# HGRN scores inside a 128-token tile: two full-width matmuls and four masked copies against seven matmuls of 32 stationary columns and one masked copy

## The chip, the cores and the metric

The kernel runs on one core of one Trainium2 chip. The metric is the device time of one execution in microseconds (us). Engines are named as the profile names them: PE is TensorE's matmuls, PEld its weight loads, DVE VectorE, ACT ScalarE, POOL GpSimd, SP SyncE, which only issues DMAs. A matmul holds a stationary operand (up to 128 columns, loaded by a weight load) and streams a moving operand past it; an output row of the matmul belongs to a stationary column, an output column to a moving column.

## The reference, cut to what matters

One decoder layer over 512 tokens: an input projection split over a gated linear recurrence (HGRN2, 4 heads of 128) and a block attention (MoBA), an output projection, cross-attention, a squared-ReLU MLP. The change touches only the HGRN2 heads:

```python
HGRN_CHUNK = 32
b = jnp.cumsum(gc, axis=3)                  # log decay inside a chunk of 32 tokens
q_t = qc * jnp.exp(b)
k_t = kc * jnp.exp(-b)
k_end = kc * jnp.exp(b_last - b)
A = jnp.where(causal, jnp.einsum('bhncd,bhnsd->bhncs', q_t, k_t), 0.0)
o_intra = jnp.einsum('bhncs,bhnsv->bhncv', A, vc)
decay = jnp.exp(b_last[..., 0, :])
def step(state, xs):
    q_n, k_n, v_n, dec_n = xs
    o_n = jnp.einsum('bhcd,bhdv->bhcv', q_n, state)
    new_state = dec_n[..., None] * state + jnp.einsum('bhsd,bhsv->bhdv', k_n, v_n)
    return new_state, o_n
```

## The kernel before, in words

**Tiles and heads.** A chunk is 32 tokens, and the kernel groups four chunks to a tile of 128 tokens, so a head has NT = 4 tiles. Inside a tile, the recurrence between its four chunks is unrolled into scores: a source token s and a target token c of the same tile have a score that goes into AT (source in the partitions, target in the columns). For a target in the source's own chunk the score is `kt` (k_t) against q_t; for a later chunk it is `kend` (k_end, kept in the buffer `Fz`) against q_t times the decay of the chunks in between. The states S pass from tile to tile only.

**What a head does.** `hgrn_pre` makes `kt`, `kend` and the small decay tables (`dc`, `ee`, `pp`, `ss`, `dt`). `ev_q` takes the projected queries of a head out of PSUM and makes, for each pair of tiles g, the buffer `qx[g]`: 128 columns of q_t per tile, and behind them copies of the later chunks' queries that are already multiplied by one or two decays, 224 columns per tile in all. `hgrn_out` is a Python generator whose pieces are the steps between its `yield`s: it transposes `ke` (tile `ket`, copied to `kets` by ACT), then makes the scores, then the tile states `pd` and `S`, then the outputs `ho`, and then normalises them (`osq`, `osh`, `osl`, `on`).

**The scores before.** Per tile there is one matmul of `kt` (128 stationary columns) against 128 columns of q_t, into the tile `a1`, and one of `kend` (128 stationary columns) against the 192 columns `32:224` of `qx`, into `a2`; the profile shows both tiles as `a`. All operands are float32, and the profile records each such matmul as two weight loads and two matmul passes. Four masked copies pick the valid blocks into AT, which was zeroed once at the start: one over all four tiles of `a1` with the mask `m0`, and for each pair of tiles three of `a2` with the masks `m1`, `m2`, `m3`, so 1 + 2 x 3 = 7 DVE instructions (COPY_PREDICATED) per head. The four masks are columns of `cst`, a 128x448 constant that ACT's queue loads from memory.

**What sets the order.** All big projections (`hf`, `hi`, `hq`, `mv`, `mkq`, `hg`, `wo`, `xq`, `xo` and the MLP's `X` and `Y`) go through `mm`, which issues one matmul and, after every 4 of them (GAP), calls `pump`: it looks for a waiting generator whose inputs are ready and issues one piece of it, up to its next `yield`. "Ready" is judged by `Pace`, a bookkeeping of estimated costs in the kernel's own Python: a float32 matmul is charged 0.215 us or 0.00168 us per moving column, whichever is more, and an input counts as ready when it is done by that bookkeeping and 2.5 us more have passed (SLACK). So the order of instructions on every engine is fixed when the program is built. The weights of a projection are split into a high part `wh` (ACT) and a low part `wl` (DVE) two units ahead of their use (SPLIT_AHEAD).

**On the lines.** Nearly every instruction is issued through one helper, L118, so the profile's groups are told apart by the names of tiles.

Of the kernel before, what the change touches and what calls it, by code (L numbers as in the profile page):

```python
# [7 lines left out]

F32 = mybir.dt.float32
F32R = mybir.dt.float32r  # L10
I32 = mybir.dt.int32
# [4 lines left out]
P = 128  # L16
# [7 lines left out]
CHUNK = 32  # L24
# [3 lines left out]
C_MASK, C_M0, C_M1, C_M2, C_M3, C_END = 0, 128, 256, 352, 416, 448  # L28
# [97 lines left out]
def hybrid_layer(ctx: ExitStack, tc: tile.TileContext, xT, memT, ws, vecs, consts, rots, out):  # L126
    nc = tc.nc
    pace = Pace()
    V, A, PE = (pace.engine(e, t) for e, t in ((nc.vector, "dve"), (nc.scalar, "act"), (nc.tensor, "pe")))
# [8 lines left out]
    fp = first.enter_context(tc.tile_pool(name="first", bufs=1, reuse_waits="tile"))  # L138
# [6 lines left out]
    def s8(dtype, name):  # L145
        return sp.tile([P, 4, T], dtype, tag="s8", name=name, bufs=N8)
# [3 lines left out]
    def s2(dtype, name, shape=(T,)):  # L150
        if name.startswith(EARLY2):
            return ep.tile([P, *shape], dtype, tag="e2", name=name, bufs=N2E)
        return sp.tile([P, *shape], dtype, tag="s2", name=name, bufs=N2)
# [14 lines left out]
    def side_bank(name):  # L168
        return pside.tile([P, T], F32, tag="ps", name=name)
# [263 lines left out]
    def start(g, key, wait=0.0):  # L433
        rec = [g, None, key]
        made[key] = rec
        side.append(rec)
        set_wait(rec, wait)
# [22 lines left out]
    def drain(key):  # L460

        rec = made[key]
        n = 0
        while any(r is rec for r in side):
            step(rec)
            n += 1
            assert n < 1000, key

    def smm(o, l, r, start=True, stop=True):

        PE.matmul(o, l, r, start=start, stop=stop, skip_group_check=True)

    def transpose(o, i):
        PE.transpose(o, i, ident)
# [64 lines left out]


    vec = cpool.tile([P, V_END], F32, name="vec")
    cst = fp.tile([P, C_END], F32, name="cst")
    rot = fp.tile([P, 2, T], F32, name="rot")
    cmask = fp.tile([P, T], F32, name="cmask")
    scan_mask = fp.tile([P, T], F32, name="scan_mask")
# [13 lines left out]
    def by_k(t):  # L559
        return t.rearrange("p (h k c) -> p h k c", h=HEADS, k=2)  # L560
# [30 lines left out]
    nc.gpsimd.memset(eps, EPS)  # L591
    make_identity(nc, ident)
    nc.gpsimd.tensor_copy(ones_r, ones)
    ATs = []
    for i in range(2):
        t = fp.tile([P, NT, P], F32, name=f"AT{i}")
# [62 lines left out]
    for k in range(5, KT):  # L659
        square_x(k)  # L660
    del raws[0]
    A.dma_start(cst, consts)
    A.dma_start(cmask[:, T - P:], consts[:, C_MASK:C_MASK + P])
    A.dma_start(rot[:32], rots)

    def rsqrt_of(dst, src, div):

        A.activation(dst, src, AF.Ln, bias=eps, scale=1.0 / div)
        A.activation(dst, dst, AF.Exp, scale=-0.5)

    def column_sums(ps, src, n, name, later=None):

        hi, lo = s2(F32R, f"{name}h"), s2(F32R, f"{name}l")
        A.activation(hi[:, :n], src, AF.Copy)
        V.tensor_sub(lo[:, :n], src, hi[:, :n].bitcast(F32))
        yield [lo[:, :n]]
        if later:
            yield later
        smm(ps[:, :n], ones_r, hi[:, :n], True, False)
        smm(ps[:, :n], ones_r, lo[:, :n], False, True)  # L680
# [45 lines left out]
    for k in range(KT):  # L726
# [7 lines left out]
        for hs in ((0, 1), (2, 3)) if k == 0 else ((0,), (1,), (2,), (3,)):  # L734
            w = {h: [by_k(t[k // 2])[:, h, k % 2] for t in (his, los)] for h in hs}
# [11 lines left out]

    Vh = s8(F32, "Vh")
    on = s8(F32, "on")
    m0 = cst[:, C_M0:C_M0 + P].bitcast(I32)  # L750
    m1 = cst[:, C_M1:C_M1 + 96].bitcast(I32)
    m2 = cst[:, C_M2:C_M2 + 64].bitcast(I32)
    m3 = cst[:, C_M3:C_M3 + 32].bitcast(I32)
    lnf = s8(F32, "lnf")
    A.activation(lnf, Fz, AF.Ln)
    head = {}
# [45 lines left out]
    def hgrn_out(h, qx, q4):  # L802
        H = head[h]
        kt, kend, ke, dt_ = H["kt"], H["kend"], H["ke"], H["dt"]
        AT = ATs[h % 2]

        yield [ke]
        pt = side_bank("ket")
        for t in range(3):
            transpose(pt[:, t * P:(t + 1) * P], ke[:, t * P:(t + 1) * P])  # L810
        ket = s2(F32, "kets")
        A.activation(ket[:, :3 * P], pt[:, :3 * P], AF.Copy)
        yield [qx[0][:, :, :P], qx[1][:, :, :P]]
        pa = side_bank("a1")
        for t in range(NT):
            smm(pa[:, t * P:(t + 1) * P], kt[:, t * P:(t + 1) * P], qx[t // 2][:, t % 2, 0:P])
        V.copy_predicated(AT, m0[:, None, :].to_broadcast([P, NT, P]), pa.rearrange("p (t c) -> p t c", c=P))
        for g in range(2):
            yield [qx[g]]
            pb = side_bank("a2")  # L820
            for t in range(2 * g, 2 * g + 2):
                smm(pb[:, (t % 2) * 192:(t % 2 + 1) * 192], kend[:, t * P:(t + 1) * P], qx[g][:, t % 2, 32:224])
            pv = pb[:, :384].rearrange("p (t c) -> p t c", c=192)
            for m, a, w, c in ((m1, 0, 96, 32), (m2, 96, 64, 64), (m3, 160, 32, 96)):
                V.copy_predicated(AT[:, 2 * g:2 * g + 2, c:], m[:, None, :].to_broadcast([P, 2, w]), pv[:, :, a:a + w])
        yield [ket[:, :3 * P]]
        pd = side_bank("pd")
        for t in range(3):
            smm(pd[:, t * P:(t + 1) * P], ket[:, t * P:(t + 1) * P], Vh[:, t, h * P:(h + 1) * P])
        S = s2(F32, f"S{h}")  # L830
        A.activation(S[:, :P], pd[:, :P], AF.Copy)
        for t in range(1, 3):
            V.scalar_tensor_tensor(S[:, t * P:(t + 1) * P], S[:, (t - 1) * P:t * P], dt_[:, t:t + 1],
                                   pd[:, t * P:(t + 1) * P], op0=ALU.mult, op1=ALU.add)
        yield [S[:, :3 * P], AT, q4]
        po = side_bank("ho")
        for t in range(NT):
            smm(po[:, t * P:(t + 1) * P], Vh[:, t, h * P:(h + 1) * P], AT[:, t, :], True, t == 0)
            if t:
                smm(po[:, t * P:(t + 1) * P], S[:, (t - 1) * P:t * P], q4[:, t * P:(t + 1) * P], False, True)  # L840
        sq = s2(F32, "osq")
        A.activation(sq, po, AF.Square)
        pn = side_bank("on")
        yield from column_sums(pn, sq, T, "os")
        rsqrt_of(sq, pn, P)
        V.tensor_mul(on[:, h, :], po, sq)
# [11 lines left out]
    def ev_q(h, acc):  # L858
        drain(("pre", h))
        H = head[h]  # L860
        qx = [s2(F32, f"qx{g}", (2, 224)) for g in range(2)]
        rbeb = H["rbeb"].rearrange("p (t c) -> p t c", c=P)
        av = acc.rearrange("p (t c) -> p t c", c=P)
        q4 = s2(F32, "q4")
        for g in range(2):
            t0 = 2 * g
            q = qx[g]
            V.tensor_mul(q[:, :, :P], av[:, t0:t0 + 2], rbeb[:, t0:t0 + 2])
            V.tensor_mul(q[:, :, P:P + 64].rearrange("p t (c s) -> p t c s", s=CHUNK),
                         q[:, :, 64:P].rearrange("p t (c s) -> p t c s", s=CHUNK),  # L870
                         H["dc"][:, t0:t0 + 2, 1:3, None].to_broadcast([P, 2, 2, CHUNK]))
            V.tensor_mul(q[:, :, P + 64:P + 96], q[:, :, 96:P],
                         H["ee"][:, t0:t0 + 2, 1:2].to_broadcast([P, 2, CHUNK]))
            V.tensor_mul(q4[:, t0 * P:(t0 + 2) * P].rearrange("p (t c s) -> p t c s", c=4, s=CHUNK),
                         q[:, :, :P].rearrange("p t (c s) -> p t c s", s=CHUNK),
                         H["pp"][:, t0:t0 + 2, :, None].to_broadcast([P, 2, 4, CHUNK]))
        start(hgrn_out(h, qx, q4), ("out", h))

    fm_stage(u, x_act, T, ev_q, "hq", ONE * 4)
    u += 4  # L880

# [474 lines left out]
    g = [s8(F32, f"g{i}") for i in range(8)]  # L1356
# [263 lines left out]
    for p, (name, begins, after) in enumerate(PLAN):  # L1620
# [3 lines left out]
        for j in range(8):  # L1624
            i, c, n = 8 * p + j, j // 4, j % 4
# [114 lines left out]
```

## Time and profile before

| | |
|---|---|
| time, median of 3 runs (lowest, highest) | 729.71 us (729.28, 729.94) |
| the profiled execution's own time | 729.77 us |
| its span (first to last recorded work) | 727.7 us |
| granted TensorE clock | 0.996 |
| PE busy | 719.3 us (99%), 4210 recorded matmul passes |
| PEld busy | 636.6 us (87%) |
| DVE busy | 573.0 us (79%) |
| ACT busy | 445.9 us (61%) |
| POOL busy | 80.9 us (11%) |

Busy PE time is the union of modelled matmul spans, and neighbouring matmuls overlap in it. What a matmul really occupies is read from the distance between the starts of neighbouring rows of the timeline. The HGRN heads' scores lie between 60 and 127 us of the span; the float32r matmuls of `hq` and `mv` run around them.

### The profile page before, as it was taken

The numbers are of one execution on the slowest core, as the hardware profiler recorded it, in microseconds if no ns is written. First come the engines' busy times: TensorE is split into PE (matmuls) and PEld (weight loads), VectorE is DVE, ScalarE is ACT, GpSimd is POOL, SyncE is SP. The second block draws the span as 40 slices with busy tenths as digits, with TensorE's granted clock in tenths as the row PEclk, the third lists the DMA queues.
The fourth block names the chain that finished last, engine by engine and source line by source line (L and its number), as shares of the span: only waits on it lengthen the run. The fifth ranks groups of instructions, "written<-read, shape, count | busy, mean of one in ns | idle before, by whom it ended". The sixth has DMA issues, their size and how long they took to land.

```text
span 727.7 us, 11176 instructions
## 1 busy us (share of the span) xinstructions
PE 719.3 (99%) x4210; PEld 636.6 (87%) x4210; DVE 573.0 (79%) x932; ACT 445.9 (61%) x676; POOL 80.9 (11%) x96
## 2 busy tenths in 40 slices
PE   9999999999999999999999999999999999999996
PEld 7888888888888888888888999999999888888885
DVE  6799556999888677677578888787888899987885
ACT  7882458455787577666565755556546655546672
POOL 1421222000000000000011111211011100110000
PEclk9999999999999999999999999999999999999998
DMA  9999689974557865463758587899889975998523
GB/s 297 285 293 309 151 169 216 363 255 127 136 176 207 250 204 174 152 196 116 232 126 162 146 205 197 216 254 264 255 227 262 318 264 179 279 274 252 181 79 116
DMA packets 63989, 155.84 MB, mean 214 GB/s; under 512 B 5280, under 2 KB 21152, under 8 KB 63424
## 3 DMA queue, kind: packets, MB, share of 16 engines
q1 hardware_dynamic: 47920, 116.43, 45.9%
q0 software_dynamic: 14592, 37.75, 28.6%
q10 hardware_dynamic: 1424, 0.95, 0.4%
q8 instruction: 33, 0.54, 0.3%
q14 instruction: 20, 0.16, 0.1%
HBM read 153.02 MB, written 48.23 MB: 277 GB/s over the span
## 4 chain that ended last, share of the span: by engine, by line
PE 97%; DMA 1%; DVE 0%; SPq 0%; ACT 0%; DVEq 0%; issue 0%
PE X L118 25%; PE Y L118 19%; PE xo L118 8%; PE mkq L118 6%; PE xq L118 6%; PE wo L118 6%; PE hg L118 3%; PE mv L118 3%; PE memX L118 3%; PE hq L118 3%; PE hi L118 3%; PE hf L118 2%; PE memY L118 2%; PE xs L118 2%; PE a L118 1%; PE po L118 1%
## 5 line engine op out<-in xcount | busy, mean ns | idle before, releaser
L118 DVE TENSOR_TENSOR wl<-wr,wh 128x1024 fp32r<-128x1024 f32 (+1 forms) x138 | 165.8, 1205 | 35.4 <-ACT wh L118 25.6
L118 ACT ACTIVATE wh<-wr 128x1024 fp32r<-128x1024 f32 (+1 forms) x138 | 142.7, 1042 | 73.7 <-DMA wr<-in_ws_dram 17.2
L236 POOL DMA_DIRECT2D u<-in_ws_dram x32 | 28.6, 893 | 353.4 <-PE memX L118 108.6
L118 PE MATMUL X<-op,wh 128*128 128x512 f32 (+1 forms) x264 | 62.9, 385 | 0.0
L118 PEld LDWEIGHTS X<-op,wh 128*128 128x128 f32 x264 | 47.2, 189 | 8.4
L118 PE MATMUL Y<-op,wh 128*128 128x512 f32 x192 | 47.2, 391 | 0.0
L118 PE MATMUL Y<-OS,wh 128*128 128x256 f32 x256 | 47.0, 283 | 0.0
L118 PE MATMUL X<-OS,wh 128*128 128x256 f32 x256 | 46.4, 283 | 0.0
L118 PEld LDWEIGHTS Y<-op,wh 128*128 128x128 f32 x192 | 35.0, 189 | 6.5
L118 PEld LDWEIGHTS Y<-OS,wh 128*128 128x128 f32 x256 | 40.0, 192 | 0.0
L118 PEld LDWEIGHTS X<-OS,wh 128*128 128x128 f32 x256 | 39.9, 192 | 0.0
L118 ACT ACTIVATE g<-t 128x512 f32<-128x512 f32 x32 | 19.0, 625 | 30.7 <-DVE t L118 30.7
L118 PE MATMUL X<-OS,wl 128*128 128x256 f32 x128 | 36.2, 283 | 0.0
L118 PE MATMUL Y<-OS,wl 128*128 128x256 f32 x128 | 36.2, 283 | 0.0
L118 PEld LDWEIGHTS X<-op,wl 128*128 128x128 f32 x256 | 33.5, 191 | 1.7
L118 PE MATMUL X<-op,wl 128*128 128x256 f32 x256 | 34.1, 282 | 0.0
L118 DVE TENSOR_TENSOR op<-g,op 128x1024 fp32r<-128x1024 f32 x24 | 29.3, 1220 | 2.8 <-ACT op L118 2.8
L118 ACT ACT_TABLE_LOAD x22 | 28.2, 1283 | 4.2 <-issue 1.8
L118 ACT ACTIVATE op<-g 128x1024 fp32r<-128x1024 f32 x28 | 29.3, 1045 | 0.5 <-PE X L118 0.5
L118 ACT ACTIVATE t<-X 128x256 f32<-128x256 f32 x32 | 11.3, 376 | 27.3 <-PE X L118 27.2
L118 PEld LDWEIGHTS Y<-op,wl 128*128 128x128 f32 x192 | 25.3, 191 | 1.3
L118 PE MATMUL Y<-op,wl 128*128 128x256 f32 x192 | 25.7, 282 | 0.0
(349 smaller groups left out, 2076.3 us busy)
## 6 DMA issues: line engine op xcount, KB each, us to landing
wr<-in_ws_dram SPq DMA_DIRECT2D x87, 512.0 KB, 5.4
u<-in_ws_dram POOLq DMA_DIRECT2D x32, 512.0 KB, 7.0
wr<-u SPq DMA_DIRECT2D x32, 512.0 KB, 4.6
u<-in_ws_dram SPq DMA_DIRECT2D x16, 512.0 KB, 10.5
wr<-m SPq DMA_DIRECT2D x16, 512.0 KB, 3.5
m<-in_ws_dram POOLq DMA_DIRECT2D x12, 512.0 KB, 8.8
m<-in_ws_dram POOLq DMA_DIRECT2D x16, 256.0 KB, 5.9
wA<-in_ws_dram SPq DMA_DIRECT2D x8, 512.0 KB, 5.5
```

The source lines that it names most:

```text
L118: return f(*args, **kw)
L236: return nc.gpsimd.dma_start(dst, src, accum_op=ALU.add, max_dma_last_dim=4 * D)
```

## The change

The scores of a tile are cut by bands of 32 source tokens. Each of the four chunks c of a tile has its own matmul of `kt`'s 32 columns, which writes the 32 partitions of that chunk in one tile `a`: columns from the tile's start to the end of chunk c, so 32, 64, 96 and 128 moving columns. The first three chunks have a second matmul, of `kend`'s 32 columns, which writes the same 32 partitions for the later chunks, with 96, 64 and 32 moving columns. In the program each of these carries a tile size of 128 rows by 32 columns and the column position 0, 32, 64 or 96 of its partitions; every other matmul of the program is 128 by 128. So a tile has seven matmuls, a head 28, and all of a head's are issued in one piece together with the three transposes of `ket`. One masked copy per head then takes the whole of `a` under the mask `causal`, which POOL makes at the start (a memset and a select); `cst` and its load are gone, and so are the six narrow masked copies per head.

`qx` is 256 columns per tile, with the twice-decayed queries of the last chunk in its last 32 columns, so that the three blocks which chunk 0 needs lie at equal distances.

```diff
+    make_upper_triangular(nc, causal, 1.0, diag=True)
...
-    A.dma_start(cst, consts)
...
-        yield [ke]
+        yield [ke, qx[0], qx[1]]
...
-        yield [qx[0][:, :, :P], qx[1][:, :, :P]]
-        pa = side_bank("a1")
+        pa = side_bank("a")
         for t in range(NT):
-            smm(pa[:, t * P:(t + 1) * P], kt[:, t * P:(t + 1) * P], qx[t // 2][:, t % 2, 0:P])
+            q = qx[t // 2][:, t % 2].rearrange("p (a s) -> p a s", s=CHUNK)
+            for c in range(4):
+                rows, own = slice(c * CHUNK, (c + 1) * CHUNK), slice(t * P + c * CHUNK, t * P + (c + 1) * CHUNK)
+                smm(pa[rows, t * P:own.stop], kt[:, own], q[:, :c + 1])
+            for c in range(3):
+                rows, own = slice(c * CHUNK, (c + 1) * CHUNK), slice(t * P + c * CHUNK, t * P + (c + 1) * CHUNK)
+                smm(pa[rows, own.stop:(t + 1) * P], kend[:, own], q[:, c + 1::3][:, :3 - c])
         V.copy_predicated(AT, m0[:, None, :].to_broadcast([P, NT, P]), pa.rearrange("p (t c) -> p t c", c=P))
-        for g in range(2):
-            yield [qx[g]]
-            pb = side_bank("a2")
-            for t in range(2 * g, 2 * g + 2):
-                smm(pb[:, (t % 2) * 192:(t % 2 + 1) * 192], kend[:, t * P:(t + 1) * P], qx[g][:, t % 2, 32:224])
-            pv = pb[:, :384].rearrange("p (t c) -> p t c", c=192)
-            for m, a, w, c in ((m1, 0, 96, 32), (m2, 96, 64, 64), (m3, 160, 32, 96)):
-                V.copy_predicated(AT[:, 2 * g:2 * g + 2, c:], m[:, None, :].to_broadcast([P, 2, w]), pv[:, :, a:a + w])
...
-        qx = [s2(F32, f"qx{g}", (2, 224)) for g in range(2)]
+        qx = [s2(F32, f"qx{g}", (2, 2 * P)) for g in range(2)]
...
-            V.tensor_mul(q[:, :, P + 64:P + 96], q[:, :, 96:P],
+            V.tensor_mul(q[:, :, P + 96:], q[:, :, 96:P],
```

On PE, at the first head's scores during the projection `hq` of the third head, the order before (`a` from `kt` for pairs of tiles; the matmuls from `Fz` come later, in two more pieces, after `hq` matmuls each):

```order
L118 MATMUL ket<-ident,ke_546 128x128 x3
L118 MATMUL hq_761<-xlo_127,wh_631 128x512
L118 MATMUL hq_761<-xhi_125,wl_632 128x512
L118 MATMUL hq_761<-xhi_125,wh_631 128x512
L118 MATMUL hq_761<-xlo_127,wh_631 128x512
L118 MATMUL a_791<-qx_694,kt_439 128x128 x2
L118 MATMUL a_791<-qx_695,kt_439 128x128 x2
L118 MATMUL hq_761<-xhi_125,wl_632 128x512
```

and the order now, up to the end of the first tile's scores; 21 more matmuls of the same form, of the other three tiles, follow before the next `hq` matmul:

```order
L118 MATMUL hq_764<-xhi_124,wl_644 128x512
L118 MATMUL ket<-ident,ke_549 128x128 x3
L118 MATMUL a<-qx_697,kt_442 32x32
L118 MATMUL a<-qx_697,kt_442 32x64
L118 MATMUL a<-qx_697,kt_442 32x96
L118 MATMUL a<-qx_697,kt_442 32x128
L118 MATMUL a<-qx_697,Fz 32x96
L118 MATMUL a<-qx_697,Fz 32x64
L118 MATMUL a<-qx_697,Fz 32x32
```

The three pieces of a head (two tiles' worth of `Fz` matmuls in each of the last two) have become one piece of 3 transposes and 28 matmuls, with no `hq` matmul inside it, and it stands some 13 `hq` matmuls earlier in the third head's projection.

On DVE, at the first head's masked copies, the order before (`AT_152` is the first head's, `AT_154` the second's; `S` are the tile states, `wl` a weight's low part, `qx` and `q` the third head's queries):

```order
L118 COPY_PREDICATED AT_152<-cst,a_791 128x512
L118 TENSOR_TENSOR qx_798<-hq_761,eb_568 128x2x128
L118 TENSOR_TENSOR wl_892<-wr_709,wh_891 128x1024
L118 TENSOR_TENSOR qx_798<-qx_798,dc_603 128x2x64
L118 TENSOR_TENSOR qx_798<-qx_798,ee_599 128x2x32
L118 TENSOR_TENSOR q_800<-qx_798,pp_600 128x256
L118 TENSOR_TENSOR qx_799<-hq_761,eb_568 128x2x128
L118 COPY_PREDICATED AT_152<-cst,a_821 128x2x96
```

and the order now (`AT_156` is the first head's, `AT_158` the second's):

```order
L118 COPY_PREDICATED AT_156<-causal,a 128x512
L118 SCALAR_TENSOR_TENSOR S_815<-S_815,dt_477,pd 128x128 x2
L118 COPY_PREDICATED AT_158<-causal,a 128x512
L118 TENSOR_TENSOR wl_995<-wr_712,wh_994 128x1024
L118 TENSOR_TENSOR osl<-osq,osh 128x512
L118 TENSOR_TENSOR qx_884<-hq_764,eb_571 128x2x128
```

The second head's masked copy now stands right behind the first head's states and ahead of the third head's queries, with a weight's split and the first head's normalisation queued behind it.

More of the change, by code (lines that the diff above doesn't have):

```diff
@@ L6 @@
 from concourse._compat import with_exitstack
-from concourse.masks import make_identity
+from concourse.masks import make_identity, make_upper_triangular
 F32 = mybir.dt.float32
@@ L541, in hybrid_layer @@
     vec = cpool.tile([P, V_END], F32, name="vec")
-    cst = fp.tile([P, C_END], F32, name="cst")
+    causal = fp.tile([P, P], F32, name="causal")
     rot = fp.tile([P, 2, T], F32, name="rot")
@@ L749, in hybrid_layer @@
     on = s8(F32, "on")
[L750 to L753, printed above, removed]
+    m0 = causal.bitcast(I32)
     lnf = s8(F32, "lnf")
```

## The prediction

> **What bounds the kernel now.** First the page's busy times and its chain of work that ended last, then that chain in order of time, and then what PE waited for.
>
> ```profile
> PE 719.3 (99%) x4210; PEld 636.6 (87%) x4210; DVE 573.0 (79%) x932; ACT 445.9 (61%) x676; POOL 80.9 (11%) x96
> ```
>
> ```profile
> PE 97%; DMA 1%; DVE 0%; SPq 0%; ACT 0%; DVEq 0%; issue 0%
> ```
>
> ```profile
> 3.15 6.32 DMA wr<-in_ws_dram
> 10.59 1.24 DVE wl L118
> 11.87 13.70 PE hf L118 x59
> ```
>
> ```profile
> PE warm L118 <- POOL eps L591: 1.0, 1, 1.0
> PE hf L118 <- DVE wl L118: 0.2, 1, 0.2
> ```
>
> After 11.9 us the path is PE alone, and the two waits PE has in all are over by then. So the time is a sum of PE issue distances, and the other engines count only where they would make PE wait. The stretch with the HGRN heads, by the windows view (columns PE, PEld, DVE, ACT, POOL, clock, DMA share, GB/s), leaves DVE a third of its time free:
>
> ```profile
> 60.00:127.00 67.00, 67.00 (x366) 58.01 (x365) 42.52 (x98) 35.49 (x48) 14.06 (x13) 1.00 0.87 206
> ```
>
> **The price of a pass.** PE's timeline at the first head's scores (start, length, and the matmuls of one row):
>
> ```profile
> 67.81 1.05 PE L118 MATMUL a<-qx,kt 128*128 128x128 f32 x8
> 68.62 0.47 PE L118 MATMUL hq<-xhi,wl 128*128 128x512 f32 x1
> 68.93 0.39 PE L118 MATMUL hq<-xhi,wh 128*128 128x512 f32 x1
> 69.16 0.39 PE L118 MATMUL hq<-xlo,wh 128*128 128x512 f32 x1
> 69.39 0.40 PE L118 MATMUL hq<-xhi,wl 128*128 128x512 f32 x1
> 69.63 0.82 PE L118 MATMUL a<-qx,Fz 128*128 128x192 f32 x4
> 70.15 0.52 PE L118 MATMUL hq<-xhi,wh 128*128 128x512 f32 x1
> 70.51 0.40 PE L118 MATMUL hq<-xlo,wh 128*128 128x512 f32 x1
> ```
>
> An `hq` matmul takes 0.23 us from start to start (68.93, 69.16, 69.39). From the start of the eight `kt` passes to the second `hq` behind them are 1.12 us; less one `hq`, 0.89 / 8 = 111 ns per pass of 128 moving columns. For the `Fz` passes 70.51 - 69.63 - 0.23 = 0.65, / 4 = 162.5 ns at 192 columns. The difference, 51.5 ns for 64 columns, is 0.80 ns per moving column, and I extend that line downwards: 85 ns at 96 columns, 60 at 64, 34 at 32.
>
> **Part 1, the scores on PE, removed and added.** Before, a tile takes two passes of each kind, 2 x 111 + 2 x 162.5 = 547 ns; 16 tiles (4 heads of 4) make 8.75 us. Now a tile streams 32 + 64 + 96 + 128 + 96 + 64 + 32 = 512 columns, against 320, in 14 passes. One round of the seven is 2 x 34 + 2 x 60 + 2 x 85 + 111 = 469 ns, and the two rounds of passes 938. What no row of before shows is how much of this runs at the same time, since every matmul in it takes the whole width. The ends:
>
> - Nothing overlaps: 16 x 0.938 = 15.0 us, so +6.3 us.
> - The four bands of 32 columns work fully by themselves: each band streams 128 columns per round, for instance 2 x (34 + 85) = 238 ns in a tile; 16 x 0.238 = 3.8 us, so -4.9 us.
> - Matmuls start in program order, each as soon as its own band is free: the second pass of a matmul waits for the first (same band), but the first pass of the next matmul (another band) starts beside that second pass. Two run at a time, and a tile takes one round, 469 ns: 16 x 0.469 = 7.5 us, so -1.25 us.
>
> I take the third, because every row of PE's timeline before starts in program order and nothing suggests that it would do so less here. [...] All bands here use all 128 rows. [...]
>
> ```profile
> L118 PEld LDWEIGHTS a<-qx,kt x32: 187/192/193, 67.6 to 102.5; 128*128 128x128 f32 x32
> L118 PE MATMUL a<-qx,kt x32: 271/275/275, 67.8 to 102.6; 128*128 128x128 f32 x32
> ```
>
> A load of 192 ns and a pass of 275 fit into 111 ns per pair, so loads do run beside passes. What a load would cost if the bands undid that is the fourth case, below.
>
> **Part 2, changing the array's shape.** Each head's burst now changes from 128x128 to 128x32 and back, 8 changes in all. The trace has only changes of data type, and they cost nothing beyond the 111 ns above: that is the lower bound, 0. Upper bound: a pass is recorded at 275 ns but handed on after 111, so 164 ns of it is a tail that the next pass normally covers. If a change has to let it run out, and then load weights with nothing beside it (111 ns more, what a pair takes), it costs 275 ns. I take the tail alone, 164 ns: 8 x 0.164 = +1.3 us; the ends are 0 and 2.2. [...]
>
> **Part 3, the masked copies.** By the groups of DVE in 60 to 130 us (count, busy us, mean ns, idle time before them) and by the waits of the whole span:
>
> ```profile
> L118 DVE COPY_PREDICATED AT<-cst,a 128x192 f32<-128x192 int32 x8 | 3.0, 375 | 2.8 <-PE a L118 2.8
> L118 DVE COPY_PREDICATED AT<-cst,a 128x512 f32<-128x512 int32 x4 | 3.0, 742 | 5.2 <-PE a L118 5.2
> L118 DVE COPY_PREDICATED AT<-cst,a 128x128 f32<-128x128 int32 x8 | 2.4, 299 | 0.2
> L118 DVE COPY_PREDICATED AT<-cst,a 128x64 f32<-128x64 int32 x8 | 1.8, 226 | 0.2
> ```
>
> ```profile
> DVE AT L118 <- PE a L118: 8.0, 7, 3.0
> ```
>
> The 24 narrow copies, 3.0 + 2.4 + 1.8 = 7.2 us of DVE, go; the four wide ones stay. DVE is not on the path and PE waits for none of it, so this is worth 0. What remains is a wait of DVE for the whole burst, with a weight's `wl` (1.2 us) behind it, by the order shown; that weight is used two units later, over 10 us at 24 `hq` matmuls of 0.23 us each. Cost 0; if the cover failed, PE would wait for one `wl`, 1.2 us, at one place.
>
> **Part 4, the order.** The kernel's own bookkeeping charges the burst 28 x 0.215 = 6.0 us, and by my sum it takes about 2. So what follows is issued up to 4 us too early, against a margin of 2.5. The nearest reader is `pd`, four `hq` behind the burst: 1.9 + 0.3 + 0.9 = about 3 us after the transposes, and it needs ACT's copy `kets`:
>
> ```profile
> 67.07 0.49 ACT L118 ACTIVATE kets<-ket 128x384 f32<-128x384 f32 x1 [3.75 <-PE ket L118]
> 89.97 0.47 ACT L118 ACTIVATE kets<-ket 128x384 f32<-128x384 f32 x1
> ```
>
> For the first head ACT stood waiting 3.75 us for it, so the copy is in time. For a later one ACT came to it from other work, and there PE could wait; I put 0 and at most 1 us.
>
> **Part 5, the start.** The load of `cst` is issued at 15.9 us, after the DMA wait of PE's path had ended, and POOL's two small operations come behind `ones_r` and `eps`, which PE's first matmuls need:
>
> ```profile
> 15.92 0.35 ACTq L118 DMA_DIRECT2D cst<-in_consts_dram  x1
> 1.43 0.28 POOL L593 CAST ones_r<-ones 128x128 fp32r<-128x128 f32 x1
> ```
>
> Both are worth 0.
>
> **Sum.** -1.25 + 1.3 = +0.05 us on the profiled execution's 729.77 us (727.7 of span and 2.1 around it): 729.8. The median of the three runs is 0.06 below that execution, so 729.8 stands for either. With the change of shape between 0 and 2.2 and up to 1 us of waits this case runs from 728.5 to 731.7. A measurement of this kernel tells about 0.2%, 1.5 us, from no change: this is "the same".
>
> **The rivals.**
>
> *One after the other* (slower). The bands do not run together, and 512 columns simply replace 320: +6.3, and the changes of shape 1.3: 737.4 us. For it: every recorded matmul before took PE alone, and the line of 0.80 ns per column holds between the two shapes there are. It decides early: with the changes of shape at 1.3, a tile that takes more than 0.56 us instead of 0.469 already puts the sum beyond 1.5 us (16 x (0.56 - 0.547) + 1.3); with free changes of shape the point is 0.64 us.
>
> *Bands by themselves* (faster). The seven matmuls spread over four bands with 128 columns each: -4.9 + 1.3 = -3.6, 726.1 us; 724.8 if a change of shape is free. For it: the four bands are evenly filled, and no data passes between them. Against it: starts in program order. [...]
>
> *A pass has a floor* (slower). Four matmuls with one moving column each show what a pass costs when it streams nothing:
>
> ```profile
> 31.83 0.95 PE L118 MATMUL nc<-ident,rb 128*128 128x1 f32 x8
> 32.64 0.47 PE L118 MATMUL hi<-wh,xlo 128*128 128x512 f32 x1
> 32.95 0.39 PE L118 MATMUL hi<-wh,xhi 128*128 128x512 f32 x1
> ```
>
> (32.95 - 31.83 - 0.23) / 8 = 111 ns, as much as with 128 columns. Those passes load 128 stationary columns. If it is the load's columns that cost, 32 of them cost a quarter, and nothing changes; if it is the pair of instructions, or a load that finds no cover, the 224 passes take 224 x 0.111 = 24.9 us, +16.1, and with the changes 747 us. [...]
>
> That the change does not do what it says is not a rival: the bands carry their own column positions in the program.
>
> **How the numbers follow.** Chances: the forecast 0.42, one after the other 0.28, bands by themselves 0.20, the floor 0.08, waits behind a burst that cost over 1.5 us 0.02. The forecast's case gives "same" 0.35, and its ends 0.05 slower and 0.02 faster. So faster 0.20 + 0.02 = 0.22, the same 0.35, slower 0.28 + 0.08 + 0.02 + 0.05 = 0.43. The likeliest single case is the forecast, 729.8 us with its own range 728.5 to 731.7; the range has to reach to both neighbours, from 725.5 (between the two ends of the bands by themselves) to 738.0 (one after the other, with half of the dearer change of shape). It leaves out the floor and a little at each end.
>
> **What would show it.** In the timeline after, the first `hq` start behind a burst tells all: the burst of 28 matmuls (56 passes) spans about 1.9 us from its first start if two run at a time, 1.0 if the bands run by themselves, 3.75 one after the other, 6.2 with the floor. A change of shape shows as a gap of about 0.16 us ahead of the burst's first pass and of the `hq` behind it. DVE's busy time should fall by 7 us. PE should show no wait for `kets`, `S` or AT; one over 1.5 us would make part 4 wrong.

## The result and the profile after

The changed kernel takes 725.53 us (median of 6 runs, 724.92 to 726.31) against 729.83 us for the kernel before (6 runs, 729.28 to 730.39). The ratio is 0.9942 with a 95% interval of 0.9929 to 0.9955: faster by 0.58%, or 4.3 us. The forecast had been no change, 729.8 us. (In the repeat of the changed kernel further down, one execution of five took 1188.4 us at a granted clock of 0.557; its ratio is that of the other four.)

The page after: the busy times, and the shares of the chain that ended last.

```profile
PE 714.9 (99%) x4370; PEld 631.5 (87%) x4370; DVE 567.2 (78%) x908; ACT 443.6 (61%) x674; POOL 81.4 (11%) x98
...
PE 99%; DVE 0%; ACT 0%; DVEq 0%; issue 0%; POOL 0%; POOLq 0%
```

PE is the whole path, as it was. It has 160 more recorded passes (224 of the narrow scores for 64 wide ones) and is busy 4.4 us less. DVE is busy 5.8 us less. All that PE waited for is the start; the wait of 0.2 us of `hf` for `wl`, which the kernel before had there, is not in this profile:

```profile
PE warm L118 <- POOL eps L591: 1.0, 1, 1.0
```

PE's timeline at the second head's scores (start, length, matmuls of one row; a row joins neighbours that use the same tiles and prints the shape of its first, so a row of several `kt` passes can hold several widths):

```profile
68.13 0.49 PE L118 MATMUL ket<-ident,ke 128*128 128x128 f32 x3
68.55 0.32 PE L118 MATMUL a<-qx,kt 128*32 128x32 f32 x5
68.64 0.25 PE L118 MATMUL a<-qx,Fz 128*32 128x96 f32 x1
68.64 0.28 PE L118 MATMUL a<-qx,kt 128*32 128x64 f32 x2
68.69 0.22 PE L118 MATMUL a<-qx,Fz 128*32 128x64 f32 x1
68.70 0.27 PE L118 MATMUL a<-qx,kt 128*32 128x128 f32 x1
68.72 0.26 PE L118 MATMUL a<-qx,Fz 128*32 128x96 f32 x4
...
68.95 0.26 PE L118 MATMUL a<-qx,Fz 128*32 128x96 f32 x4
...
69.18 0.26 PE L118 MATMUL a<-qx,Fz 128*32 128x96 f32 x4
...
69.59 0.51 PE L118 MATMUL hq<-xhi,wh 128*128 128x512 f32 x1
69.93 0.40 PE L118 MATMUL hq<-xlo,wh 128*128 128x512 f32 x1
70.17 0.40 PE L118 MATMUL hq<-xhi,wl 128*128 128x512 f32 x1
```

Three things can be read here. The rows 68.72, 68.95 and 69.18 are the same place in three neighbouring tiles: a tile takes 0.23 us (0.228 by the single records of the trace, which the rows join). The burst, from the first score at 68.55 to the `hq` start at 69.59, is 1.04 us; the prediction had listed 1.0 for bands by themselves and 1.9 for two at a time. And the starts are not in program order: the program has all eight `kt` passes of a tile ahead of its first `Fz` pass, but one `Fz` pass starts after five of them, and the other three `kt` passes start later. The single records of the first tile show the bands side by side (start in ns after 68.550):

```
band 0:  0 (32 columns)   53 (32)    85 (96)   170 (96)   next tile 253
band 1:  7 (64)           87 (64)   143 (64)   199 (64)   next tile 255
band 2: 14 (96)          120 (96)   203 (32)   231 (32)   next tile 263
band 3: 20 (128)         154 (128)                        next tile 263
```

Each band goes through its own list at its own pace.

**The sum after.** From the start of `ket` to the second `hq` behind it are 69.93 - 68.13 = 1.80 us. Less one `hq`, 0.23, and less the transposes (before, by the two rows below, 67.12 - 66.55 - 0.23 = 0.34), the burst with both changes of shape costs 1.23 us per head. Before, a head paid 0.89 + 0.65 + 0.65 = 2.19 us for the same scores. The difference, 4 x 0.96 = 3.8 us, is what the scores save on PE by this sum. The rows of before, in its timeline:

```profile
66.55 0.49 PE L118 MATMUL ket<-ident,ke 128*128 128x128 f32 x3
66.79 0.49 PE L118 MATMUL hq<-xlo,wh 128*128 128x512 f32 x1
67.12 0.39 PE L118 MATMUL hq<-xhi,wl 128*128 128x512 f32 x1
```

Of the 1.23 us, four tiles are 0.91; I put the other 0.32 down to the two changes of shape, 0.16 each on average.

The two timelines also give the gain whole. These are the first `hq` matmul and the first `X` matmul, before and then after; all the scores lie between them:

```profile
51.36 0.39 PE L118 MATMUL hq<-xhi,wh 128*128 128x512 f32 x1
400.66 0.40 PE L118 MATMUL X<-OA,wh 128*128 128x256 f32 x2
...
50.85 0.39 PE L118 MATMUL hq<-xhi,wh 128*128 128x512 f32 x1
396.09 0.40 PE L118 MATMUL X<-OA,wh 128*128 128x256 f32 x2
```

From `hq` to `X` are 349.30 us before and 345.24 after, 4.06 less (345.29 in the repeat of the changed kernel). So the sum of 3.8 misses about 0.25 us of this stretch. The other 0.5 us by which the changed kernel's profile is ahead were there before the first `hq`, and no score had run by then.

### The profile page after: what moved, and what is told of

Its sections match the earlier page's. It is cut to its first block, busy times and chain, and to the rows that moved or that the text cites. A ratio compares the mean times of both kernels' runs of the same rounds, so it can differ in the third digit from the quotient of the medians.

```text
span 723.1 us, 11459 instructions
## 1 busy us (share of the span) xinstructions
PE 714.9 (99%) x4370; PEld 631.5 (87%) x4370; DVE 567.2 (78%) x908; ACT 443.6 (61%) x674; POOL 81.4 (11%) x98
## 4 chain that ended last, share of the span: by engine, by line
PE 99%; DVE 0%; ACT 0%; DVEq 0%; issue 0%; POOL 0%; POOLq 0%
PE X L118 25%; PE Y L118 19%; PE xo L118 8%; PE mkq L118 6%; PE xq L118 6%; PE wo L118 6%; PE hq L118 3%; PE hf L118 3%; PE hg L118 3%; PE mv L118 3%; PE memX L118 3%; PE hi L118 3%; PE memY L118 2%; PE xs L118 2%; PE sc L118 1%; PE po L118 1%
```

## The experiments

**One band.** Theory A: the four bands work side by side. Rival B: a narrow pass is cheap by itself. Rival C: the gain is not PE's.

```diff
-                rows, own = slice(c * CHUNK, (c + 1) * CHUNK), slice(t * P + c * CHUNK, t * P + (c + 1) * CHUNK)
+                rows, own = slice(0, CHUNK), slice(t * P + c * CHUNK, t * P + (c + 1) * CHUNK)
...
-        V.copy_predicated(AT, m0[:, None, :].to_broadcast([P, NT, P]), pa.rearrange("p (t c) -> p t c", c=P))
+        V.copy_predicated(AT[:CHUNK], m0[:CHUNK, None, :].to_broadcast([CHUNK, NT, P]), pa[:CHUNK].rearrange("p (t c) -> p t c", c=P))
```

The second loop's `rows` (the three dots) is changed in the same way.

> All seven matmuls of a tile write the same 32 partitions, so they all use the first column band of the array; everything else, the order of instructions included, stays as in the changed kernel. Only the first band's scores reach AT, so the scores of the other three bands are left out. Theory A (the four bands of 32 columns work side by side, each at its own pace, so a tile takes as long as its longest band, 0.228 us in the changed kernel's trace): without other bands the passes queue, 14 passes of about 28, 56, 86 or 110 ns are 0.90 us per tile, 16 x (0.90 - 0.228) = 10.8 us more than the changed kernel, 736.3 us. Rival B (a pass of 32 stationary columns is simply cheap, because its weight load is a quarter): the same 725.5 us as the changed kernel. Rival C (the gain comes from the copies or from the start, not from TensorE): 725.5 us too.

Measured: 736.41 us (736.09 to 737.46), 1.0097 of the kernel before (1.0080 to 1.0114). The first burst, in PE's timeline:

```profile
63.88 0.75 PE L118 MATMUL a<-qx,kt 128*32 128x32 f32 x8
64.47 0.50 PE L118 MATMUL a<-qx,Fz 128*32 128x96 f32 x6
64.80 0.72 PE L118 MATMUL a<-qx,kt 128*32 128x32 f32 x8
...
67.59 0.50 PE L118 MATMUL hq<-xhi,wh 128*128 128x512 f32 x1
```

Now the eight `kt` passes come before the six `Fz` passes. The first tile takes 0.92 us (63.88 to 64.80), each later one 0.90 by the single records, and the burst 3.71. The order of instructions on PE is the changed kernel's; only the band differs, and with it the partitions that are written. So B and C fall: without the four bands the same passes are 6.7 us slower than the kernel before. Going from one band to four makes a tile about 4 times as fast (0.90 against 0.228 us).

**Two bands.**

```diff
-                rows, own = slice(c * CHUNK, (c + 1) * CHUNK), slice(t * P + c * CHUNK, t * P + (c + 1) * CHUNK)
+                rows, own = slice(c % 2 * CHUNK, (c % 2 + 1) * CHUNK), slice(t * P + c * CHUNK, t * P + (c + 1) * CHUNK)
...
```

The second loop's `rows` is changed in the same way, and the masked copy takes the first 64 partitions alone.

> Chunks 0 and 2 write the first 32 partitions, chunks 1 and 3 the second 32, so two of the four bands work; the scores of the upper two bands are left out of AT. If a tile takes its longest band: 2 x (28 + 86 + 86 + 28) = 456 ns, twice the changed kernel's, 16 x 0.228 = 3.65 us more, 729.3 us. If two bands already carry all that the array takes at once (four bands are no better than two): 725.6 us. If less than two bands' worth runs together: up to the 736.4 us of the run with one band.

Measured: 729.24 us (728.79 to 729.57), 0.9995 (0.9985 to 1.0004). In PE's timeline of the first burst:

```profile
64.11 0.53 PE L118 MATMUL a<-qx,kt 128*32 128x32 f32 x8
...
66.05 0.50 PE L118 MATMUL hq<-xhi,wh 128*128 128x512 f32 x1
```

The burst is 1.94 us. So the time follows the longest band's list, 1.04, 1.94 and 3.71 us for four, two and one.

**The bands outermost.** How far ahead does PE look?

```diff
-        for t in range(NT):
-            q = qx[t // 2][:, t % 2].rearrange("p (a s) -> p a s", s=CHUNK)
-            for c in range(4):
+        for c in range(4):
+            for t in range(NT):
+                q = qx[t // 2][:, t % 2].rearrange("p (a s) -> p a s", s=CHUNK)
...
-            for c in range(3):
+                if c < 3:
```

> The same 28 matmuls per head, but the four tiles of band 0 first, then those of band 1, 2, 3: 8 matmuls, 16 passes, stand in one band before the next band's first. Theory A with a look-ahead that reaches all 56 passes: each band starts at once, the burst stays 1.0 us, 725.5 us. Theory A with starts in program order (a pass can't start before the one ahead of it has): the bands run one after the other, 4 x 4 x 0.228 = 3.65 us per head, 10.4 us more, 736 us. A look-ahead of a few passes lies between, and the starts of band 1 against the end of band 0 in the trace give its depth.

Measured: 734.00 us (733.47 to 734.38), 1.0059 (1.0044 to 1.0074): neither end. In PE's timeline of the first burst:

```profile
63.74 0.25 PE L118 MATMUL a<-qx,kt 128*32 128x32 f32 x2
63.82 0.33 PE L118 MATMUL a<-qx,Fz 128*32 128x96 f32 x2
...
64.44 0.25 PE L118 MATMUL a<-qx,kt 128*32 128x32 f32 x3
64.50 0.25 PE L118 MATMUL a<-qx,Fz 128*32 128x96 f32 x1
64.53 0.22 PE L118 MATMUL a<-qx,kt 128*32 128x64 f32 x1
64.59 0.28 PE L118 MATMUL a<-qx,Fz 128*32 128x64 f32 x3
...
66.85 0.50 PE L118 MATMUL hq<-xhi,wh 128*128 128x512 f32 x1
```

The row of 64 columns at 64.53 is band 1's second pass; it starts before band 0's last, so a band does start ahead of the program's order, but only late in the other's list. The single records show how late. Bands 0, 1 and 2 have 16 passes each here, and the next band's first pass starts 6 ns after the 13th of the band ahead of it: 715 after 709 ns, 1415 after 1409, 2126 after 2120. Each time three passes of the band ahead had not started: in this run a band started when 13 of the 16 passes of the band ahead had. What held it until then, no trace shows. The burst is 3.12 us, 4 x (3.12 - 1.04) = 8.3 us more than the changed kernel; measured are 8.5 more.

**Band by band inside a tile.** The edge of what was seen there: four passes of one band in a row.

```diff
             for c in range(4):
...
                 smm(pa[rows, t * P:own.stop], kt[:, own], q[:, :c + 1])
-            for c in range(3):
-                rows, own = slice(c * CHUNK, (c + 1) * CHUNK), slice(t * P + c * CHUNK, t * P + (c + 1) * CHUNK)
-                smm(pa[rows, own.stop:(t + 1) * P], kend[:, own], q[:, c + 1::3][:, :3 - c])
+                if c < 3:
+                    smm(pa[rows, own.stop:(t + 1) * P], kend[:, own], q[:, c + 1::3][:, :3 - c])
```

> Inside each tile both matmuls of a band stand together (four passes of band 0, then four of band 1, four of band 2, two of band 3), tile after tile. The run with the bands outermost showed band 1 starting when three passes of band 0 ahead of it had not started yet. If that is the rule (each band holds up to three passes that wait, and only a fourth one holds up what stands behind it): four passes of a band hold up nothing, the tile stays at 0.228 us and the burst at 1.04, 725.6 us. If passes start in program order, as the prediction had it: about 0.62 us per tile, 16 x 0.39 = 6.3 us more, 731.9 us.

Measured: 726.34 us (725.48 to 726.38), 0.9950 (0.9933 to 0.9966). In PE's timeline of the first burst:

```profile
64.62 0.34 PE L118 MATMUL a<-qx,kt 128*32 128x32 f32 x5
...
65.73 0.50 PE L118 MATMUL hq<-xhi,wh 128*128 128x512 f32 x1
```

The burst is 1.10 us, 0.06 more than expected. By the single records band 0 keeps its 228 ns per tile, but in every tile one pass of band 3 is followed by the next only after 132 to 134 ns; in the changed kernel, from band 3's second pass on, that is 109 to 110. So its last pass starts 94 ns later than there: four in a row do hold band 3 up a little. The rest of the 0.7 us over the expected time is within the interval; the profile has two short waits of PE ahead of all scores, 0.5 us (`hf` for `wl`) and 0.4 (`hq` for `Vh`), in a part that the edit does not touch. Program order is out by 5.6 us.

**Four pieces.**

```diff
                 smm(pa[rows, own.stop:(t + 1) * P], kend[:, own], q[:, c + 1::3][:, :3 - c])
+            if t < NT - 1:
+                yield [qx[t // 2]]
```

> A head's burst is cut into four pieces, one per tile, with four projection matmuls between them: 24 more changes of the array's shape in all. If a change costs the tail of a pass, 0.164 us: +3.9 us, 729.5 us, and all of the change's gain is gone. If a change is free and the 0.32 us around a burst are something that a head pays once: 725.5 us.

Measured: 729.79 us (729.61 to 730.19), 1.0002 (0.9993 to 1.0011), so the cuts eat the whole gain. In PE's timeline:

```profile
65.01 0.39 PE L118 MATMUL hq<-xhi,wl 128*128 128x512 f32 x1
65.24 0.39 PE L118 MATMUL hq<-xhi,wh 128*128 128x512 f32 x1
65.56 0.32 PE L118 MATMUL a<-qx,kt 128*32 128x32 f32 x5
...
65.91 0.50 PE L118 MATMUL hq<-xlo,wh 128*128 128x512 f32 x1
66.25 0.40 PE L118 MATMUL hq<-xhi,wl 128*128 128x512 f32 x1
```

From 65.24 to 66.25 are 1.01 us for two `hq` (0.46) and one tile (0.23): 0.32 for two changes of shape. By the single records it is lost in three places: 0.09 ahead of the first score, 0.13 between the last tile's time and the next `hq`, 0.11 behind that `hq`.

**All passes narrow.** The scores of chunks two and three apart are left out.

```diff
-                smm(pa[rows, t * P:own.stop], kt[:, own], q[:, :c + 1])
+                smm(pa[rows, own], kt[:, own], q[:, c])
...
-                smm(pa[rows, own.stop:(t + 1) * P], kend[:, own], q[:, c + 1::3][:, :3 - c])
+                smm(pa[rows, own.stop:own.stop + CHUNK], kend[:, own], q[:, c + 1])
...
-        V.copy_predicated(AT, m0[:, None, :].to_broadcast([P, NT, P]), pa.rearrange("p (t c) -> p t c", c=P))
+        pv = pa.rearrange("p (t c) -> p t c", c=P)
+        for c in range(4):
+            rows, cols = slice(c * CHUNK, (c + 1) * CHUNK), slice(c * CHUNK, min(P, (c + 2) * CHUNK))
+            V.copy_predicated(AT[rows, :, cols], m0[rows, None, cols].to_broadcast([CHUNK, NT, cols.stop - cols.start]), pv[rows, :, cols])
```

> All seven matmuls of a tile stream 32 columns only (each band its own chunk and the next one), so scores two and three chunks apart are left out; four masked copies per head take what is there. The longest band has 2 x 2 passes of about 28.5 ns, 0.114 us per tile. Theory A (the longest band): 16 x 0.114 = 1.8 us less than the changed kernel, 723.7 us. If 14 passes per tile are bound by their issue, 16 ns each: no difference, 725.5 us.

Measured: 724.57 us (724.20 to 724.85), 0.9930 (0.9915 to 0.9945), between the two expectations, and its interval overlaps the changed kernel's. The trace is sharper than the time: the burst is 0.64 us, so the bands' lists did get shorter.

```profile
64.21 0.27 PE L118 MATMUL a<-qx,kt 128*32 128x32 f32 x8
...
64.35 0.24 PE L118 MATMUL a<-qx,kt 128*32 128x32 f32 x7
64.42 0.24 PE L118 MATMUL a<-qx,Fz 128*32 128x32 f32 x6
64.48 0.26 PE L118 MATMUL a<-qx,kt 128*32 128x32 f32 x8
...
64.61 0.26 PE L118 MATMUL a<-qx,kt 128*32 128x32 f32 x8
...
64.84 0.50 PE L118 MATMUL hq<-xhi,wh 128*128 128x512 f32 x1
```

A tile takes 0.13 us (64.35, 64.48, 64.61), four passes per band of about 32 ns each; 14 passes in 0.13 us leave 9 ns for the issue of one. So an issue of 16 ns per pass is not the bound. 4 x 0.40 = 1.6 us should be gained on the changed kernel; the time shows 1.0, which with the width of these intervals is no contradiction, and PE's trace from the first `hq` to the first `X` shows it: 343.57 us against 345.24, 1.67 less.

**The changed kernel again, the load, the copies.** Is the gain PE's alone?

> The changed kernel once more, to stand beside the three variants of this job: 725.5 us, ratio to the kernel before 0.994.

Measured: 725.65 us (median of all five), 0.9944 (0.9931 to 0.9958).

```diff
+    cst = fp.tile([P, C_END], F32, name="cst")
...
+    A.dma_start(cst, consts)
```

> The changed kernel with the 128x448 constant still loaded at its old place (nothing reads it). In the two profiles, the changed kernel's PE is 0.5 us ahead before its first score. If that comes from the missing load: 0.5 us slower than the changed kernel, 726.0 us. If it is how two executions start: no difference, 725.5 us.

Measured: 725.75 us (724.85 to 726.38), 0.9945 (0.9932 to 0.9957): no difference that can be told, though intervals of about 0.9 us to either side would hide 0.5. The profiles say more. The first matmul of `hi` starts at 28.65 us in the profile of before, 28.15 and 28.37 in two profiles of the changed kernel, 28.20 to 28.84 in the eight other profiles without the load, and 29.21 here. So the 28.65 of before lies within what executions without the load show, and the head start can be chance; but the two profiles with the load have a mean of 28.93 against 28.49, so a few tenths for the load are not excluded.

```diff
+        pv = pa.rearrange("p (t c) -> p t c", c=P)
+        for g in range(2):
+            for w, c in ((96, 32), (64, 64), (32, 96)):
+                V.copy_predicated(AT[:, 2 * g:2 * g + 2, c:], m0[:, None, c:].to_broadcast([P, 2, w]), pv[:, 2 * g:2 * g + 2, c:])
```

> The changed kernel with six more narrow masked copies per head, of the widths that were removed (they copy the same scores once more). Theory A (the copies stand beside PE and are worth nothing): 725.5 us. Rival C (the gain is DVE's): up to 4 us slower, 729.5 us.

Measured: 725.48 us (725.17 to 726.21), 0.9942 (0.9930 to 0.9955). Its page has DVE where it was before, at the changed kernel's time:

```profile
PE 715.3 (99%) x4370; PEld 632.4 (87%) x4370; DVE 573.0 (79%) x932; ACT 443.2 (61%) x674; POOL 81.3 (11%) x98
```

So the "one masked copy per head" of the change is worth nothing that can be told here.

**Two heads in one burst.** What the runs point to is fewer changes of shape. The scores of heads 0 and 1, and of 2 and 3, are issued together:

```diff
+    def pair_scores(heads):
+        yield [t for h, qx, q4 in heads for t in (head[h]["ke"], qx[0], qx[1])]
...
+        for h, qx, q4 in heads:
+            kt, kend = head[h]["kt"], head[h]["kend"]
+            pa = side_bank("a")
...
-        start(hgrn_out(h, qx, q4), ("out", h))
+        heads_q.append((h, qx, q4))
+        if h % 2:
+            start(pair_scores(heads_q[-2:]), ("sc", h))
```

> The scores of two heads in one burst of 56 matmuls, so four changes of the array's shape instead of eight. If a change costs 0.164 us: 0.66 us less than the changed kernel, 724.9 us. If the larger burst makes PE wait for the second head's queries or leaves something late behind it: more than 725.5 us.

Measured: 729.08 us (728.26 to 730.85), 0.9992 (0.9983 to 1.0001): the gain is gone. The first pair does what was expected (its burst is 1.96 us, against 2 x 1.04 and one more pair of changes), but PE now waits:

```profile
PE a L118 <- DVE on L118: 1.6, 1, 1.6
PE mkq L118 <- DVE Vml L118: 1.2, 1, 1.2
PE warm L118 <- POOL eps L591: 1.0, 1, 1.0
PE a L118 <- ACT osq L118: 0.6, 1, 0.6
```

1.6 + 1.2 + 0.6 = 3.4 us of waits, far more than the 0.66 us that fewer changes of shape were to save; it is 3.4 us slower than the changed kernel's repeat. Two of the waits stand ahead of the scores of the second pair's two heads: the readers of the first pair's `ho` had not finished when the next `a` was to be written. That the four side banks of PSUM run out there is my reading of it and was not tested. No version here that does all of the work is measurably faster than the changed kernel.

## Why the prediction was wrong

**What bounds the kernel: right.** PE alone carried the path before and after, and the gain is, but for some tenths, a sum of PE's distances. The measured 725.53 us stands at the very end of the whole range, which reached down to 725.5 for the sake of the rival *bands by themselves*; the forecast's own case ended at 728.5.

**Part 1 failed**, at the step "I take the third": matmuls starting in program order, two at a time, 469 ns per tile. The trace shows 228 ns and starts out of that order; with the bands outermost a band started when 13 of the 16 passes of the band ahead had, and in the kernel's own order no band is left without work (the records above: each band's passes follow each other without a break). The step's reason was that every row of before starts in program order. That was no evidence: every matmul of the program before takes all 128 columns, so none of its rows could show what passes of different bands do beside each other. The prediction's own middle case (a second band starts only when the first begins its second pass) could not be told from the fully parallel one by any row of before, and should have weighed no more than it.

Starts in program order are not what the trace of these bands shows: an `Fz` pass starts at 68.64 us, ahead of three `kt` passes that the program has before it. Nor do the weight loads show as time of their own: all bands use all 128 rows, a load is recorded at 106 to 114 ns, and 14 loads and 14 passes fit into 228 ns. And the bands do run beside each other: four take 0.228 us for what one band does in 0.90.

The terms around it were sized well. The line of 0.80 ns per column gave 34, 60, 85 and 111 ns; the records of the bands give 28 to 32, 56, 82 to 86 and 110, but for each band's first pass of a burst (53, 80, 106 and 134). The longest band came to 238 ns by it, measured 228. One band alone was put at 938 ns, measured 0.90 us.

**Part 2: right in size.** 8 x 0.164 = 1.3 us was forecast; four bursts at 0.32 are 1.3, and cutting each burst into four cost 4.3 us where 24 x 0.164 is 3.9. But the cost does not fall as forecast, as two gaps of 0.16: it is 0.09 ahead of the burst, 0.13 ahead of the `hq` behind it and 0.11 behind that `hq`. That it is the tail of a pass running out was the prediction's estimate, and no run shows it. **Part 3: right,** the copies are worth nothing that can be told; DVE's busy time fell by 5.8 us instead of 7. **Part 4: right,** no wait of PE came. **Part 5: not contradicted,** no cost of the load was measured, within about 0.9 us.

**The rivals.** *Bands by themselves* was the case that happened, at 726.1 us against 725.53; its burst of 1.0 us is the 1.04 in the trace. It had 0.20. Its sum of -3.6 is -3.8 with the measured 228 ns, and the runs say -4.3 with an interval of -5.2 to -3.3. So the times do not resolve the 0.5 us between. In the traces, about 0.25 us more than the sum are gained between the first `hq` and the first `X`, and the two profiles differ by 0.5 us before the first `hq`. I give no cause for either. *One after the other*, at 737.4, is what one band does, 736.41. *The floor* is out: within one band the next pass starts 28 to 32 ns after one of 32 columns (53 after a burst's first) and not 111, and the burst takes 1.04 us and not 6.2.

## What to carry to other kernels

Where a float32 matmul needs few output rows, try cutting its stationary columns into four bands of 32, each with its own output partitions. Here the bands ran side by side (0.228 us per tile against 0.90 in one band), and the burst went with the longest band's list (1.04, 1.94 and 3.71 us with four, two and one); so price it by that list and not by the sum of the columns. Issue the bands in turn: here four passes of one band in a row cost 0.06 us per burst, sixteen cost 2.1 us, and nothing between was tried. Put them in as few bursts as bring no waits: each burst cost 0.32 us here beyond its tiles, which I put down to changing the array's shape and back, and cutting four bursts into sixteen cost 4.3 us; but two heads in one burst brought 3.4 us of waits. And when the trace of before holds nothing that can tell two mechanisms apart, its silence is no argument for the one in the middle.

## What the runs showed of the hardware that was not expected

- Four column bands give about four times the rate: 0.90 us per tile in one band, 0.228 in four; the burst is 3.71, 1.94 and 1.04 us with one, two and four bands.
- With the bands outermost, the next band's first pass starts 6 ns after the 13th of the 16 ahead of it, three times in a row.
- Passes of different bands start 6 to 7 ns apart at the start of a burst; within one band the next pass starts 28 to 32 ns after one of 32 columns, 53 after the burst's first.
